# A two-layer hybrid decoder trunk on one core: the next layer's norm one step behind its residual, table transfers with weight loads between them, the norm row loaded ahead of the constants, and a new order of jobs

## The chip, the core and the metric

The kernel runs on one core of a Trainium2 chip. A core has five engines that each execute their own list of instructions in order: TensorE (PE, matmuls; PEld in the rows is its weight load), VectorE (DVE), ScalarE (ACT), GpSimd (POOL) and SyncE (SP), which here only issues DMA transfers, all in one queue. The metric is the device time of one execution in microseconds, as the median of several runs.

## The reference

Two layers, 512 tokens, 1024 channels. Each layer normalises its input, projects it with one wide matrix `w_in`, feeds five token mixers, gates and sums them, projects with `w_out`, normalises once more and adds the result to its input:

```python
def layer(x, mem, pos, l):                          # cut to its structure
    h = rms_norm(x, norm_pre[l])
    a, b, c, d, q, gates = split(h @ w_in[l], IN_SIZES)
    y = [rwkv7_branch(a), dsa_branch(b, pos), retention_branch(c, pos),
         s5_branch(d), cross_attention(q, mem)]
    m = sum(sigmoid(g_i) * (y_i @ w_branch[l, i]) for i, ...)
    return x + rms_norm(m @ w_out[l], norm_post[l])
```

All of it is float32. The S5 branch is a diagonal complex recurrence, y = scan over t of s = lambda * s + B u; its powers of lambda are a table that depends on the weights alone.

## The kernel before, in words

Every weight matrix is streamed in pieces of 128 x 512 numbers (256 KB), 448 of them. A piece (`class Load`) is brought by SP into `raw` (5 buffers), ACT casts it to a rounded high part `wh` (4 buffers), DVE makes the rest `wl = raw - wh` (4 buffers, called the split), and PE does three matmuls for each product: high by high, low by high, high by low. Activations are held the same way, as `hh` and `hl`. `prefetch` issues transfers up to 5 pieces ahead and casts and splits up to 3 pieces ahead of the job that uses them, in the order of use.

The products are jobs with short names (`rq`, `xq`, `dv` and so on). `ORDER` (L40) lists them for each of the two layers; the mixers between them run as generators in lanes, with priorities in `LANES` (L42). When the program is built, `run()` steps through jobs and lanes with a model of the engines' clocks (`Sched`, constants `LAG`, `EARLY`, `ADD_G`) and so fixes the order in which each engine gets its instructions; on the chip nothing is reordered. A `yield` in a generator is a place at which `run()` may go on with something else.

Where layer 0 goes over to layer 1, `out_jobs` multiplies by `w_out` for tokens 0 to 255 and then 256 to 511. For each of the four tiles of 128 tokens `finish_out` makes the residual (`x<-ou,ors,x`, two halves on DVE, behind a power `ors` on POOL) and calls `put_hT` for the next layer: the sum of squares on ACT (`xn<-x`), a power on POOL (`xrs`), two products on DVE (`xn<-x,xrs,npre`), eight transposes on PE, `hh` on ACT and `hl` on DVE. The new input is also stored (`xs<-x`). Jobs of layer 1 that need only two tiles (`rq`, `rk`, `xq`, `rv`) run as half jobs as soon as these are there; a half job takes its pieces twice as fast as a whole one.

`s5_tables` makes the S5 tables of a layer. `sar` grows by doubling, seven times, with `sta`, `sea`, `seb`, `sem` as helpers; each group of three operations goes to DVE or POOL, whichever the model thinks free (`free_for`), the rest to POOL. Then four transfers `s5tab<-sar` and four loads of `sBt` go out on SP, and the loads of `sCg` follow. SP issues in order, so a transfer whose data is not there holds every later one, the weight pieces too.

At the start SP loads `x` of token tile 0, the first constants `cst`, `x` of tile 1, the norm's row `npre`, and then the first five weight pieces. `first_h` runs `put_hT` for the four tiles.

Of the kernel before, what the change touches and what calls it, by code (L numbers as in the profile page):

```python
# [31 lines left out]
CW2 = float(np.float32(np.round((TWO_PI - CW1) * 2.0 ** 21) / 2.0 ** 21))  # L32
CW3 = float(np.float32(TWO_PI - CW1 - CW2))
MAGIC = 12582912.0
LAG = 11.5
EARLY = -1.0
MAXL = 6
NBUF = {"c1": 10, "c2": 14, "c4": 16, "c16": 2, "raw": 5, "w": 4}
ADD_G = 1.2
ORDER = ("rsg rv w wg g0 xq xsg di su dsg ssg dq g4 g2 dk mem1 dv g3 mem g1",  # L40
         "xsg dq g0 w di rsg wg g4 su dsg ssg dk dv g3 g1 g2")
LANES = ("ret idx>4 s5>4 ms1>3 rwkv dsa ms0 tab x>2", "idx>4 dsa>0 tab ret x rwkv>t s5")  # L42


def shape_constants():
# [177 lines left out]
def hybrid_kernel(ctx: ExitStack, tc: tile.TileContext, x, mem, positions, norm_pre, norm_post, norm_mem, w_in,  # L223
# [17 lines left out]
    def psb(shape=(128, 512)):  # L241
        return sched.ring("b", 5, pp.tile(list(shape), F32, name="b", tag="b", bufs=5))


    def sb(name, shape, dt=F32, bufs=2, lane="c", big=False):
        n = int(np.prod(shape[1:]))
        if n <= 128 and not big:
            return bp.tile(list(shape), dt, name=name, tag=name, bufs=bufs)
        if dt == BF16:
            return bp.tile([128, 512], dt, name=name, tag="m1", bufs=3)  # L250
        if n == 4096 and dt == F32:
            return sched.ring("mg", 1, bp.tile(list(shape), dt, name=name, tag="mg", bufs=1))
        c, w = next((c, w) for c, w in ((1, 256), (2, 516), (4, 1032), (16, 4096)) if n <= w and not (big and c == 1))
        t = bp.tile([128, w], dt, name=name, tag=f"c{c}", bufs=NBUF[f"c{c}"])
        v = t[:shape[0], :n]
        if len(shape) > 2:
            names = "abcdef"[:len(shape) - 1]
            v = v.rearrange(f"p ({' '.join(names)}) -> p {' '.join(names)}",
                            **{m: k for m, k in zip(names, shape[1:])})
        return v  # L260

    def f32(ap):
        return ap.bitcast(F32)

    def bcast_row(ap, name):

        t = sb(name, [128, ap.shape[-1]])
        SY.dma_start(t, bass.AP(tensor=ap.tensor, offset=ap.offset, ap=[[0, 128], [1, ap.shape[-1]]]))
        return t
# [6 lines left out]
    def load_x(l, i):  # L276
        t = sb("x", [128, D])
        SY.dma_start(t, xr[:, i, :] if l == 0 else xs[:, i, :])
        return t

    x0 = [load_x(0, 0)]
    ncst = COFF["qdec"][0]
    cst = cp.tile([128, ncst], F32, name="cst")
    nci = COFF["ident"][1]
    assert COFF["ident"][0] == 0 and CONST.shape[1] == ncst + 1024
    SY.dma_start(cst[:, :nci], const[:, :nci])
    x0.append(load_x(0, 1))
    npre = {0: bcast_row(norm_pre[0], "npre")}

    def K(n):  # L290
        o, w = COFF[n]
# [6 lines left out]
    def rsq(dst, src):  # L298
        sh = list(src.shape)
        assert len(sh) == 2  # L300
        G.tensor_tensor(dst, src, mhalf[:sh[0], :sh[1]], op=OP.pow)
# [147 lines left out]
    def rms_scale(src, name, j):  # L449

        r = sb(name, [128, 1], bufs=4)
        A.activation(j, src, AF.Square, accum_out=r)
        V.tensor_scalar(r, r, 1.0 / D, 1e-6, op0=OP.mult, op1=OP.add)
        rsq(r, r)
        return r
# [27 lines left out]
    def new_hT(l):  # L483
        hh = sb("hh", [128, 8, S], F32R)
        hl = sb("hl", [128, 8, S], F32R)
        hT[l] = (hh, hl)

    def put_hT(l, i, xi):

        if l not in hT:  # L490
            new_hT(l)
        hh, hl = hT[l]
        xn = sb("xn", [128, D])
        r = rms_scale(xi, "xrs", xn)
        yield
        for o in (slice(0, 512), slice(512, 1024)):
            V.scalar_tensor_tensor(xn[:, o], xi[:, o], r, npre[l][:, o], op0=OP.mult, op1=OP.mult)
        yield
        for k in (0, 4):
            ps = psb((128, 4, 128))  # L500
            for kk in range(4):
                T.transpose(ps[:, kk, :], xn[:, 128 * (k + kk):128 * (k + kk) + 128], ident)
            o = (slice(None), slice(k, k + 4), slice(128 * i, 128 * i + 128))
            A.copy(hh[o], ps)
            V.tensor_tensor(hl[o], ps, f32(hh[o]), op=OP.subtract)
            yield
# [25 lines left out]
    def prefetch(upto, ahead=2):  # L532

        while len(stream) < upto + NBUF["raw"] and select():
            pass
        while lp["dma"] < min(len(stream), upto + NBUF["raw"]):
            stream[lp["dma"]].dma()
            lp["dma"] += 1
        while lp["split"] < min(lp["dma"], upto + 1 + ahead):
            stream[lp["split"]].split()  # L540
            lp["split"] += 1
# [54 lines left out]
    def select():  # L596

        left = [jb for jb in jobs if not jb.taken]
        if not left:
            return False  # L600
        lanes = [q.room for q in queue if have(q.need)][:1]

        def last(jb):
            return jb.merge is not None and sum(m == jb.merge for m in merging) == 4

        def fits(jb, spare=()):
            if jb.gate is not None and jb.gate[1] == 0 and opened:
                return False
            return room_for({"c4": 6} if last(jb) else jb.room, spare)
        if any(not t.granted for t in begun):  # L610
            return False
        able = [j for j in left if (j.after is None or j.after.taken) and have(j.need)
                and not (opened and j.gate is not None and j.gate[1] == 0)]
        jb = next((j for j in able if fits(j, lanes)), None)
        if jb is None and able:
            jb = able[0]
            if last(jb) or not all(have(q.need) for q in active):
                return False
            jb.granted = False
        elif jb is None:  # L620
            jb = left[0]
            if not fits(jb, lanes) and (active or not fits(jb)):
                return False
        jb.last = last(jb)
        begun[:] = [t for t in begun if not t.granted] + [jb]
        if jb.granted:
            grant(jb)
        if jb.merge is not None:
            merging.append(jb.merge)
        if jb.gate is not None:  # L630
            opened[:] = [jb.gate[0]] if jb.gate[1] < 3 else []
        jb.taken = True
        for w in jb.loads:
            w.idx = len(stream)
            stream.append(w)
        taken.append(jb)
        return True
# [792 lines left out]
    def s5_tables(l):  # L1430
# [5 lines left out]
        tab = [area[:, r_] for r_ in range(2)]  # L1436
# [12 lines left out]
        while m < 128:  # L1449
# [3 lines left out]
            t = tmp[:, :, :m]  # L1453
# [12 lines left out]
        for r_ in range(2):  # L1466
            for b in range(2):
                SY.dma_start(s5d["tab"][2 * l + b][:, r_], tab[r_][:, 4 * b:4 * b + 4].rearrange("p b m -> p (b m)"))

        Bt = sb("sBt", [128, 2, nb, 16])  # L1470
        Cs = sb("sCs", [128, 2, nb, 16])
        for r_, w in enumerate((s5_b_re, s5_b_im)):
            bv = w[l].rearrange("(b q) p c -> q p b c", q=2)
            for q in range(2):
                SY.dma_start(Bt[64 * q:64 * q + 64, r_], bv[q])
        yield
        for b in range(2):
# [46 lines left out]
        for b in range(2):  # L1524
# [23 lines left out]
            for j in range(4):  # L1548
                for i in range(j, 4):
                    n = 32 * (3 - (i - j))  # L1550
# [228 lines left out]
    def finish_out(l, i):  # L1779

        u, rr, xi = (a[i % 2] for a in ST[l, "fin", i // 2])
        rs = sb("ors", [128, 1])
        V.tensor_tensor(rs, rr[:, 0:1], rr[:, 1:2], op=OP.add)
        V.scalar_tensor_tensor(rs, rr[:, 2:3], 16e-6, rs, op0=OP.add, op1=OP.add)
        rsq(rs, rs)
        yield
        for a in range(2):
            o = slice(512 * a, 512 * a + 512)
            V.scalar_tensor_tensor(xi[:, o], u[:, o], rs, xi[:, o], op0=OP.mult, op1=OP.add)
            if l == L - 1:  # L1790
                yield
                SY.dma_start(outr[:, i, o], xi[:, o])
        if l < L - 1:
            yield from put_hT(l + 1, i, xi)
            SY.dma_start(xs[:, i, :], xi)

# [30 lines left out]
    def run(lanes, maxl=MAXL):  # L1827
# [3 lines left out]
        while alive or active or queue:  # L1831
# [9 lines left out]
            now = sched.clock["pe"]  # L1841
            late = max(sched.clock["dve"], sched.clock["act"]) > now + LAG
            pick = None if late and alive else next(
# [53 lines left out]
    def first_h(i):  # L1897
        if i >= 2:
            x0.append(load_x(0, i))
            yield  # L1900
        yield from put_hT(0, i, x0[i])

    lanes = [Lane(lambda i=i: first_h(i), ("t01",) if i > 1 else (), f"t0{i}", c4=2 + (i == 0)) for i in range(4)]
    lanes += [Lane(setup, ("t01",), "setup", c2=3, c4=4)]
    for l in range(L):
# [31 lines left out]
        }  # L1937
        for n in ORDER[l].split():
            if n[0] == "g":
                gate_jobs(l, int(n[1]))  # L1940
            else:
# [10 lines left out]
                    "dsa": Lane(lambda l=l: branch_dsa(l), (f"dsa_q{l}", "trig"), f"y{l}1", c1=2, c2=5, c4=2)}  # L1952
        for n in LANES[l].split():
            n, _, after = n.partition(">")
# [39 lines left out]
```

## Time and profile before

| | |
|---|---|
| median of 3 runs | 1432.06 us (1430.72 to 1433.5) |
| the profiled execution's own time | 1431.76 us |
| its span, first to last instruction | 1430.0 us |
| mean granted clock of TensorE | 0.986 of full speed |
| PE busy | 1373.7 us, 96% of the span |
| DVE busy | 950.2 us, 66% |
| ACT busy | 558.3 us, 39% |
| POOL busy | 279.1 us, 20% |
| HBM traffic | 114 GB/s over the span |

The profiled execution took 1.76 us more than its span. Busy times are sums over an engine's instructions; that PE is busy does not say at which of its two clocks (1.2 or 2.4 GHz) it ran, which the granted clock tells. Times in the rows are us from the first instruction.

### The profile page before, as it was taken

The numbers are of one execution on the slowest core, as the hardware profiler recorded it, in microseconds if no ns is written. First come the engines' busy times: TensorE is split into PE (matmuls) and PEld (weight loads), VectorE is DVE, ScalarE is ACT, GpSimd is POOL, SyncE is SP. The second block draws the span as 40 slices with busy tenths as digits, with TensorE's granted clock in tenths as the row PEclk, the third lists the DMA queues.
The fourth block names the chain that finished last, engine by engine and source line by source line (L and its number), as shares of the span: only waits on it lengthen the run. The fifth ranks groups of instructions, "written<-read, shape, count | busy, mean of one in ns | idle before, by whom it ended". The sixth has DMA issues, their size and how long they took to land.

```text
span 1430.0 us, 21718 instructions
## 1 busy us (share of the span) xinstructions
PE 1373.7 (96%) x7774; PEld 1147.8 (80%) x7774; DVE 950.2 (66%) x2027; ACT 558.3 (39%) x1196; POOL 279.1 (20%) x329
## 2 busy tenths in 40 slices
PE   5999999999999999999979899999999999999997
PEld 5878777788878887888979788687888788778887
DVE  5677565978867864444666567668788786844465
ACT  5433445333334235233554452443323332344353
POOL 0194241000111111110019523210010112411000
PEclk9999899999999999999999899999999999999999
DMA  6644425364242432344656624263534322422355
GB/s 193 176 114 127 122 89 141 89 184 126 72 121 74 129 101 52 89 118 125 188 152 177 180 78 134 60 143 94 141 103 147 89 67 72 114 67 81 99 163 181
DMA packets 243414, 170.60 MB, mean 119 GB/s; under 512 B 27657, under 2 KB 228331, under 8 KB 243307
## 3 DMA queue, kind: packets, MB, share of 16 engines
q1 hardware_dynamic: 243307, 169.22, 42.6%
q8 instruction: 61, 1.00, 0.3%
q14 instruction: 46, 0.38, 0.1%
HBM read 144.53 MB, written 18.87 MB: 114 GB/s over the span
## 4 chain that ended last, share of the span: by engine, by line
PE 82%; DVE 6%; POOL 4%; DMA 3%; ACT 2%; issue 2%; SPq 1%; POOLq 0%; DVEq 0%; ACTq 0%
PE d L209 62%; PE b L209 19%; DVE wl L209 2%; POOL sar L209 2%; DMA raw<-in_w_out_dram 1%; POOL sta L209 1%; DMA raw<-in_w_in_dram 1%; DVE x L209 1%; SPq L209 1%; ACT wh L209 0%; DMA posi<-in_positions_dram 0%; DMA x<-in_x_dram 0%; DMA rsw<-rq 0%; POOL sem L209 0%; POOL rsw L209 0%
## 5 line engine op out<-in xcount | busy, mean ns | idle before, releaser
L209 PE MATMUL d<-hh,wh 128*128 128x512 f32 (+2 forms) x1232 | 488.3, 396 | 13.5 <-ACT wh L209 13.5
L209 PE MATMUL d<-hh,wl 128*128 128x512 f32 (+2 forms) x1232 | 474.3, 385 | 6.6 <-DVE wl L209 6.5
L209 PE MATMUL d<-hl,wh 128*128 128x512 f32 (+2 forms) x1232 | 472.1, 383 | 0.0
L209 DVE TENSOR_TENSOR wl<-raw,wh 128x512 fp32r<-128x512 f32 x448 | 334.0, 761 | 139.2 <-ACT wh L209 135.6
L209 ACT CAST wh<-raw 128x512 fp32r<-128x512 f32 x448 | 268.7, 617 | 165.6 <-PE d L209 111.9
L209 PEld LDWEIGHTS d<-hh,wh 128*128 128x128 f32 (+1 forms) x1232 | 235.6, 191 | 73.1 <-issue 15.0
L209 PEld LDWEIGHTS d<-hh,wl 128*128 128x128 f32 (+1 forms) x1232 | 234.8, 191 | 58.4 <-DVE wl L209 10.1
L209 PEld LDWEIGHTS d<-hl,wh 128*128 128x128 f32 (+1 forms) x1232 | 235.8, 191 | 42.3 <-issue 0.5
L209 POOL TENSOR_TENSOR mg<-mg,gth 128x512 f32<-128x512 f32 x48 | 69.9, 1457 | 486.2 <-DVE gth L209 486.2
L209 DVE SCALAR_TENSOR_TENSOR gth<-gth,d 128x512 f32<-128x512 f32 x64 | 43.9, 686 | 107.2 <-PE d L209 103.4
L209 ACT ACTIVATE gth<-d 128x512 f32<-128x512 f32 (+1 forms) x90 | 51.9, 577 | 159.7 <-PE d L209 155.0
L209 PE MATMUL b<-wh,mgs 128*128 128x256 f32 x320 | 63.2, 283 | 5.6 <-ACT wh L209 4.1
L209 PE MATMUL d<-yl,wh 128*128 128x512 f32 x160 | 62.9, 393 | 0.7 <-DVE yl L209 0.7
L209 PE MATMUL d<-yh,wl 128*128 128x512 f32 x160 | 62.8, 393 | 0.0
L209 PE MATMUL d<-yh,wh 128*128 128x512 f32 x160 | 62.7, 392 | 0.0
L209 PEld LDWEIGHTS b<-wh,mgs 128*128 128x128 f32 x320 | 52.1, 190 | 6.3 <-ACT wh L209 4.3
L209 DVE MAX8 dm<-dac 128x8 f32<-128x256 f32 (+2 forms) x96 | 52.8, 550 | 0.1
L209 DVE MATCH_REPLACE8 dac<-dm,dac 128x256 f32<-128x256 f32 (+2 forms) x96 | 52.1, 543 | 0.0
L209 PE MATMUL b<-wl,mgs 128*128 128x256 f32 x160 | 45.5, 285 | 0.3 <-DVE wl L209 0.3
L209 POOL TENSOR_TENSOR ors<-ors,mhalf 128x1 f32<-128x1 f32 x8 | 5.0, 634 | 203.3 <-DVE ors L209 203.3
L209 PE MATMUL d<-wh,mgs 128*128 128x256 f32 x192 | 40.6, 285 | 2.0 <-DVE ou L209 2.0
L209 POOL TENSOR_TENSOR rsw<-rsw,sinT 128x1024 f32<-128x1024 f32 (+1 forms) x12 | 29.7, 2480 | 44.0 <-DMA rsw<-diq 20.7
(399 smaller groups left out, 2067.9 us busy)
## 6 DMA issues: line engine op xcount, KB each, us to landing
raw<-in_w_in_dram SPq DMA_DIRECT2D x324, 256.0 KB, 3.4
raw<-in_w_out_dram SPq DMA_DIRECT2D x64, 256.0 KB, 4.7
raw<-in_w_branch_dram SPq DMA_DIRECT2D x40, 256.0 KB, 3.2
x<-in_x_dram SPq DMA_DIRECT2D x8, 512.0 KB, 6.0
raw<-in_w_mem_kv_dram SPq DMA_DIRECT2D x16, 256.0 KB, 2.9
s5tab<-sar SPq DMA_DIRECT2D x8, 256.0 KB, 2.0
s5Wi<-sar SPq DMA_DIRECT2D x4, 512.0 KB
nn<-wNt SPq DMA_DIRECT2D x8, 256.0 KB
```

The source lines that it names most:

```text
L209: r = f(*args, **kw)
```

## The change

The module constants `LAG`, `ORDER` and `LANES` get other values, by which nearly every engine's order changes somewhere. In `s5_tables` a `yield` follows each pair of table transfers and stands ahead of each `sBt` load. In `finish_out` a `yield` stands between the residual and the norm of the next layer. At the start `npre` is loaded ahead of `cst`, and `first_h` calls `prefetch(0, 0)` in the second step of tile 1.

```diff
@@ -32,14 +32,14 @@
 CW2 = float(np.float32(np.round((TWO_PI - CW1) * 2.0 ** 21) / 2.0 ** 21))
 CW3 = float(np.float32(TWO_PI - CW1 - CW2))
 MAGIC = 12582912.0
-LAG = 11.5
+LAG = 10.5
 EARLY = -1.0
 MAXL = 6
 NBUF = {"c1": 10, "c2": 14, "c4": 16, "c16": 2, "raw": 5, "w": 4}
 ADD_G = 1.2
-ORDER = ("rsg rv w wg g0 xq xsg di su dsg ssg dq g4 g2 dk mem1 dv g3 mem g1",
-         "xsg dq g0 w di rsg wg g4 su dsg ssg dk dv g3 g1 g2")
-LANES = ("ret idx>4 s5>4 ms1>3 rwkv dsa ms0 tab x>2", "idx>4 dsa>0 tab ret x rwkv>t s5")
+ORDER = ("xq rsg rv w g1 wg g3 xsg dsg di ssg su g4 dk dq dv mem1 mem g2 g0",
+         "w xsg g1 dq di rsg dv g0 ssg su g3 g4 wg dk g2 dsg")
+LANES = ("ms1>3 tab ms0 s5 dsa>2 ret x rwkv idx>4", "ret s5>2 rwkv>4 x tab dsa>0 idx>2")
 
 
 def shape_constants():
@@ -279,13 +279,13 @@
         return t
 
     x0 = [load_x(0, 0)]
+    npre = {0: bcast_row(norm_pre[0], "npre")}
     ncst = COFF["qdec"][0]
     cst = cp.tile([128, ncst], F32, name="cst")
     nci = COFF["ident"][1]
     assert COFF["ident"][0] == 0 and CONST.shape[1] == ncst + 1024
     SY.dma_start(cst[:, :nci], const[:, :nci])
     x0.append(load_x(0, 1))
-    npre = {0: bcast_row(norm_pre[0], "npre")}
 
     def K(n):
         o, w = COFF[n]
@@ -1466,12 +1466,14 @@
         for r_ in range(2):
             for b in range(2):
                 SY.dma_start(s5d["tab"][2 * l + b][:, r_], tab[r_][:, 4 * b:4 * b + 4].rearrange("p b m -> p (b m)"))
+            yield
 
         Bt = sb("sBt", [128, 2, nb, 16])
         Cs = sb("sCs", [128, 2, nb, 16])
         for r_, w in enumerate((s5_b_re, s5_b_im)):
             bv = w[l].rearrange("(b q) p c -> q p b c", q=2)
             for q in range(2):
+                yield
                 SY.dma_start(Bt[64 * q:64 * q + 64, r_], bv[q])
         yield
         for b in range(2):
@@ -1791,6 +1793,7 @@
                 yield
                 SY.dma_start(outr[:, i, o], xi[:, o])
         if l < L - 1:
+            yield
             yield from put_hT(l + 1, i, xi)
             SY.dma_start(xs[:, i, :], xi)
 
@@ -1898,7 +1901,10 @@
         if i >= 2:
             x0.append(load_x(0, i))
             yield
-        yield from put_hT(0, i, x0[i])
+        for n, _ in enumerate(put_hT(0, i, x0[i])):
+            if n == 1 and i == 1:
+                prefetch(0, 0)
+            yield
 
     lanes = [Lane(lambda i=i: first_h(i), ("t01",) if i > 1 else (), f"t0{i}", c4=2 + (i == 0)) for i in range(4)]
     lanes += [Lane(setup, ("t01",), "setup", c2=3, c4=4)]
```

Three places show what this moves. The first is SP's queue at the layer seam: `raw` are weight pieces, `xs` the stored residuals, `s5tab` and `sBt` the table transfers and loads. Before:

```order
L209 DMA raw<-in_w_in_dram 128x4x128 x12
L209 DMA raw<-in_w_in_dram 128x2x256
L209 DMA xs<-x 128x1024 x2
L209 DMA raw<-in_w_in_dram 128x2x256 x3
L209 DMA raw<-in_w_in_dram 128x4x128 x11
L209 DMA s5tab<-sar 128x512 x4
L209 DMA sBt<-in_s_b_re_dram 64x8x16 x2
L209 DMA sBt<-in_s_b_im_dram 64x8x16 x2
L209 DMA raw<-in_w_in_dram 128x4x128
```

And now, from the same place in the program:

```order
L209 DMA raw<-in_w_in_dram 128x4x128 x8
L209 DMA raw<-in_w_in_dram 128x2x256 x3
L209 DMA xs<-x 128x1024
L209 DMA raw<-in_w_in_dram 128x2x256
L209 DMA xs<-x 128x1024
L209 DMA raw<-in_w_in_dram 128x4x128 x10
L209 DMA s5tab<-sar 128x512 x2
L209 DMA raw<-in_w_in_dram 128x4x128 x2
L209 DMA s5tab<-sar 128x512 x2
L209 DMA raw<-in_w_in_dram 128x2x256 x3
L209 DMA sBt<-in_s_b_re_dram 64x8x16
L209 DMA raw<-in_w_in_dram 128x2x256
```

Before, 27 pieces of `w_in` went out ahead of the four table transfers and none between them or the `sBt` loads. Now 26 go out ahead of the first pair (2 and 2 stand ahead of these rows), two between the pairs, three behind the second, and further ones between the `sBt` loads.

On POOL the same place begins with the power `ors` of the second half's residual; the steps of the table follow. Before:

```order
L209 TENSOR_TENSOR ors<-ors,mhalf 128x1 x2
L209 MEMSET sar 128x8 x2
L209 COPY sem<-un 128x16
L209 TENSOR_TENSOR xrs<-xrs,mhalf 128x1 x2
L209 TENSOR_TENSOR sar<-sar,sem 128x8
L209 TENSOR_TENSOR sta<-sar,sem 128x8
L209 TENSOR_TENSOR sar<-sar,sta 128x8
L209 TENSOR_TENSOR sea<-sem 128x16
L209 TENSOR_TENSOR seb<-sem 128x8 x2
```

And now:

```order
L209 COPY sem<-un 128x16
L209 TENSOR_TENSOR sar<-sar,sem 128x8
L209 TENSOR_TENSOR sta<-sar,sem 128x8
L209 TENSOR_TENSOR sar<-sar,sta 128x8
L209 TENSOR_TENSOR sea<-sem 128x16
L209 TENSOR_TENSOR seb<-sem 128x8 x2
L209 TENSOR_TENSOR sem_7221<-sea 128x8
L209 TENSOR_TENSOR sem_7221<-seb 128x8
L209 TENSOR_TENSOR xrs<-xrs,mhalf 128x1 x2
L209 TENSOR_TENSOR sar<-sar,sem_7221 128x8x2
```

Eight steps of the table, from `sar` to `sem`, moved from behind the two `xrs` powers to ahead of them. Of the next doubling one group of three steps, which was POOL's, stands on DVE now.

On DVE, at the residual of tiles 0 and 1 (the first half of the seam), `wl` is the split of a weight piece and `xrs` prepares the norm's power. Before:

```order
L209 SCALAR_TENSOR_TENSOR ors<-or,ors 128x1
L209 TENSOR_TENSOR wl<-raw,wh 128x512 x2
L209 SCALAR_TENSOR_TENSOR x<-ou,ors,x 128x512 x2
L209 TENSOR_SCALAR xrs<-xrs 128x1
L209 SCALAR_TENSOR_TENSOR x<-ou,ors,x 128x512 x2
L209 TENSOR_SCALAR xrs<-xrs 128x1
L209 TENSOR_TENSOR wl<-raw,wh 128x512 x3
L209 SCALAR_TENSOR_TENSOR xn<-x,xrs,npre 128x512 x4
```

And now:

```order
L209 TENSOR_TENSOR wl<-raw,wh 128x512 x2
L209 SCALAR_TENSOR_TENSOR x<-ou,ors,x 128x512 x4
L209 TENSOR_TENSOR wl<-raw,wh 128x512 x2
L209 TENSOR_SCALAR xrs<-xrs 128x1
L209 TENSOR_TENSOR wl<-raw,wh 128x512
L209 TENSOR_SCALAR xrs<-xrs 128x1
L209 TENSOR_TENSOR wl<-raw,wh 128x512
L209 SCALAR_TENSOR_TENSOR xn<-x,xrs,npre 128x512 x2
L209 TENSOR_TENSOR ou<-b,npost 128x512
L209 TENSOR_TENSOR ou<-d,npost 128x512
L209 TENSOR_TENSOR wl<-raw,wh 128x512
L209 SCALAR_TENSOR_TENSOR xn<-x,xrs,npre 128x512 x2
```

The two residuals stand together ahead of both `xrs`, and four splits (before, three behind them) stand between the residuals and the first norm product.

## Rows read from the trace of the kernel before

**Rows 1.** The page: busy time, share of span and instructions of each engine.

```profile
PE 1373.7 (96%) x7774; PEld 1147.8 (80%) x7774; DVE 950.2 (66%) x2027; ACT 558.3 (39%) x1196; POOL 279.1 (20%) x329
```

**Rows 2.** Waits of PE by what it waited for: total us, times, longest us.

```profile
PE d L209 <- ACT wh L209: 13.5, 4, 8.4
...
PE d L209 <- DVE wl L209: 7.2, 7, 2.2
```

**Rows 3.** Windows: length, busy us (instructions) per engine, then PEclk, DMA share, GB/s.

```profile
160.00:170.00 10.00, 10.00 (x35) 8.74 (x36) 4.50 (x7) 4.66 (x13) 4.94 (x2) 0.50 0.29 80
...
200.00:204.00 4.00, 4.00 (x14) 3.17 (x15) 2.06 (x5) 3.66 (x12) 3.80 (x6) 0.59 0.00 0
...
720.00:740.00 20.00, 19.27 (x152) 19.07 (x153) 15.38 (x27) 11.01 (x28) 0.00 (x0) 0.93 0.67 201
740.00:760.00 20.00, 16.79 (x128) 16.38 (x128) 14.74 (x30) 10.54 (x22) 12.45 (x35) 0.91 0.58 172
...
788.00:798.00 10.00, 6.03 (x27) 5.81 (x28) 4.12 (x5) 3.54 (x7) 5.34 (x9) 0.50 0.98 267
```

**Rows 4.** Timeline of SP, 700 to 800: start, us, operation, tile, count.

```profile
752.49 21.66 SPq L209 DMA_DIRECT2D raw<-in_w_in_dram  x14
779.86 5.05 SPq L209 DMA_DIRECT2D s5tab<-sar  x4
...
787.81 2.66 SPq L209 DMA_DIRECT2D raw<-in_w_in_dram  x5
```

**Rows 5.** Timeline of POOL, 740 to 790: in brackets idle time before, and releaser.

```profile
742.05 0.20 POOL L209 COPY sem<-un 128x16 f32<-128x16 f32 x1
746.75 0.98 POOL L209 TENSOR_TENSOR xrs<-xrs,mhalf 128x1 f32<-128x1 f32 x1 [4.50 <-DVE xrs L209]
749.44 0.55 POOL L209 TENSOR_TENSOR xrs<-xrs,mhalf 128x1 f32<-128x1 f32 x1 [1.71 <-DVE xrs L209]
749.95 0.52 POOL L209 TENSOR_TENSOR sar<-sar,sem 128x8 f32<-128x8 f32 x1
...
755.00 0.20 POOL L209 TENSOR_TENSOR sem<-seb 128x8 f32<-128x8 f32 x1
...
782.81 1.28 POOL L209 TENSOR_TENSOR sar<-sar,sta 128x512 f32<-128x512 f32 x1
```

**Rows 6.** Timeline of PE, 715 to 795, the rows with a wait.

```profile
719.15 0.38 PE L209 MATMUL b<-wh,mgs 128*128 128x256 f32 x1 [4.15 <-ACT wh L209]
719.87 0.58 PE L209 MATMUL b<-wl,mgs 128*128 128x256 f32 x1 [0.34 <-DVE wl L209]
...
749.73 0.39 PE L209 MATMUL d<-hh,wh 128*128 128x256 f32 x1 [2.99 <-ACT wh L209]
...
791.97 0.58 PE L209 MATMUL d<-hh,wh 128*128 128x256 f32 x1 [8.35 <-ACT wh L209]
```

**Rows 7.** Timeline of DVE at the first wait.

```profile
712.69 0.69 DVE L209 TENSOR_TENSOR wl<-raw,wh 128x512 fp32r<-128x512 f32 x1 [2.56 <-ACT wh L209]
713.30 1.41 DVE L209 SCALAR_TENSOR_TENSOR x<-ou,ors,x 128x512 f32<-128x512 f32 x2
```

**Rows 8.** Timeline of PE in layer 0, 155 to 199.

```profile
157.00 1.61 PE L209 MATMUL b<-wwa,lora 64*128 64x512 f32 x4 [1.09 <-ACT sar L209]
...
191.36 1.89 PE L209 MATMUL b<-xvm,xpT 128*128 128x64 f32 x16
...
195.86 0.50 PE L209 MATMUL d<-hh,wl 128*128 128x512 f32 x1 [0.89 <-DVE wl L209]
...
198.50 1.95 PE L209 MATMUL b<-cst,wr 128*128 128x2 f32 x16 [0.57 <-DVE xon L209]
```

**Rows 9.** Timelines of ACT, DVE and PE at the start.

```profile
7.65 1.06 ACT L209 ACTIVATE xn<-x 128x1024 f32<-128x1024 f32 x1 [1.98 <-DMA x<-in_x_dram]
...
9.11 2.74 DVE L209 SCALAR_TENSOR_TENSOR xn<-x,xrs,npre 128x512 f32<-128x512 f32 x4
...
15.32 0.58 PE L209 MATMUL d<-hh,wh 128*128 128x256 f32 x1 [1.19 <-ACT wh L209]
```

## The prediction

> **What bounds the kernel now.** I began with the page. TensorE (PE) is busy for 1373.7 of 1430.0 us [rows 1], so whatever the new order does to VectorE (DVE), ScalarE (ACT) or GpSimd (POOL) counts only where PE waits for it, or where PE works at the slower of its two clocks (1.2 instead of 2.4 GHz). The two programs hold the same matmuls, so nothing is to be had from the work itself. The list of PE's waits by releaser came next: its largest entries, behind the start, are waits for `wh`, the cast half of a weight piece, 13.5 us in 4 waits of which one alone is 8.4, and for `wl`, 7.2 us in 7 [rows 2]. The timeline puts three large ones at the layer seam: 4.15 us before 719.15 and 2.99 us before 749.73, where the residuals of token tiles 0, 1 and of 2, 3 are made, and 8.35 us before 791.97 [rows 6]. I call them the first, second and third wait. Windows then showed where the clock is low: 0.50 over 160 to 170 and over 788 to 798, where PE was busy for 6.03 of the 10 us, 0.59 over 200 to 204, and 0.93 and 0.91 around the first two waits [rows 3]. One us of work at the low clock costs 0.5 us.
>
> What makes the third wait is seen on SyncE (SP), which issues all transfers in one queue. Fourteen weight pieces went out in 21.66 us from 752.49 (about 1.5 us each), then SP stood until the table transfers of 779.86, whose four issues ended at 784.91; four `sBt` transfers followed, and the next piece left at 787.81 [rows 4]. SP stood because the table was not there: POOL's chain of doubling steps ended at 784.09 (782.81 + 1.28) [rows 5]. That chain began at 742.05, but then sat behind the two `xrs` powers of the norm, which were waiting for DVE, until 749.95 [rows 5].
>
> **The change part by part.**
>
> *Table transfers and chain.* (a) Eight steps (from `sar` at 749.95 to `sem`, ending 755.20) now stand ahead of the two `xrs`. They took 5.2 us, about 0.66 each, beside DVE's splits and norm products, although the last of them alone took 0.20 [rows 5]. Even at 0.66 they fit into the 4.50 and 1.71 us in which POOL idled [rows 5]. The chain goes on behind the second `xrs`, at 749.99, with its ninth step. Upper bound: the following steps run at 0.2, all 5.2 us are saved, and a group of three steps that goes to DVE saves 0.6 more: 5.8. Lower bound: the steps that take the freed place run beside the same splits and products and stretch the same way; then only 8 x 0.2 + 0.6 = 2.2 is gained. I take 2.2, since DVE's work behind the second `xrs` is as dense as before. (b) The weight pieces no longer stand behind `sBt`: 787.81 - 784.91 = 2.9 us. (c) The first pair of tables goes out after 26 pieces instead of 27, two pieces go before the second pair, and so one more piece reaches PE before the last hold: 1.5 us of work. Sum 2.2 + 2.9 + 1.5 = 6.6 us, and some 1.8 us of the 8.35 are left. What PE saves in the second wait arrives here as waiting, since the chain is counted from the same residual; I cost the second wait at nothing by itself (bounds 0 and 2.99). (d) After a remaining wait of two or so us I expect a low-clock stretch like that after the second wait, the 0.91 of 740 to 760, 20 x 0.09 = 1.8 us, instead of 6.03 x 0.5 = 3.0 [rows 3]: -1.2. Together -7.8.
>
> The same rows meet a rule that speaks against (a). The Trainium skill, page "SBUF — State Buffer", section "Who interferes with whom", says that a DVE instruction with two SBUF inputs contends with a GpSimd instruction that reads SBUF, and that whoever comes first holds the pair for the whole instruction. The trace agrees for POOL (0.66 beside DVE, 0.20 alone). By the rule the residual products, which have two such inputs, would in turn be held by the eight steps now beside them, 8 x 0.2 = 1.6 us; the chain would start again that much later, and the sum would be 1.6 us smaller, 1422.2. The rows can't show it, as no step stood there.
>
> *Norm one step behind its residual.* At the first wait DVE now does all four residual products before anything else. Before, the split ending at 713.38 was followed by two products of together 1.41 us, a wait for ACT's square and two more products, and PE, back at 719.15, still waited 0.34 us for the next split [rows 6, 7]. Now ACT casts six pieces ahead of its squares, and DVE's third split comes straight behind 2.8 us of products: ready at about 713.3 + 2.8 + 0.7 = 716.8. PE stopped at 719.15 - 4.15 = 715.0 and so waits 1.8 us: the gain is 4.15 + 0.34 - 1.8 = 2.7. Bounds: 0, if the norm, now behind more splits, makes PE's transposes late; 4.5 if nothing waits. The clock's 0.93 over 720 to 740 [rows 3] cost 20 x 0.07 = 1.4 us; whether it falls after the shorter wait is open, 0 to 1.4, and I take half, 0.7. At the second wait nine splits now lie between the residual and the last `hl`, where five lay, and PE takes the transposes of tiles 2 and 3 two pieces later: cover of 3 us for 4 x 0.69 = 2.8 [rows 7], so this costs nothing unless that cover is missing; then up to 2.8 us.
>
> *New order of jobs.* In layer 0 the small matmuls of RWKV, S5 tables and cross-attention fall together differently. Before: waits of 1.09, 0.89 and 0.57 us [rows 8], a window at 0.50 (5.0 us lost) and one at 0.59 (4 x 0.41 = 1.6) [rows 3]: 9.2 in all. The clock fell there beside PE busy throughout 160 to 170, after a stretch of short matmuls with single waits of about 1 us. Now there are two such clusters with no weight matmul inside. The longer holds `xp` twice, `xvm` twice, `xkm`, `wv`, `wr` and `wta`; at what the 16 matmuls of `xvm` (1.89) and of `wr` (1.95) took [rows 8], and half of that for each group of eight, that is near 10 us. The shorter is half as long. Costed like the two seen, 5.0 + 1.6, and with half the waits, 1.3 us, that is 7.9: -1.3. The page "TensorE: Matmul & The Clock Gate" of the Trainium skill, section "HAM oscillation", ties the return to the low clock to waits between matmuls. By that rule alone the long cluster would keep its clock and the sum would be 5.0 us better; the row at 157.00 shows the fall after 1.09 us, so the trace does not bear that out. The other places where lanes now meet cost something unknown: the rest of PE's waits for `wl` is 7.2 - 2.2 = 5 us [rows 2], so -5 to +5, and I put +1.
>
> *Head.* The norm row `npre` is loaded ahead of the constants, but DVE still handles `xrs` of tile 1 before the `xn` products of tile 0, and tile 1 now arrives last. The products, before at 9.11 [rows 9], thus move by up to the 1.5 us that now lie between the start of tile 1's square at 7.65 and them [rows 9]. In return the first piece is cast and split ahead of `hh` and `hl`; PE waited 1.19 us for it [rows 9]. I cost the head at 0 (bounds -1.2, +1.5).
>
> Sum: -7.8 - 2.7 - 0.7 - 1.3 + 1 + 0 = -11.5. The profiled execution took 1431.76 us (1430.0 of span and 1.76 around it), so 1420.3; the median of the runs lies 0.3 us above it: **1420.6 us**.
>
> **The rivals.** 0.2%, what a measurement can tell from no change here, is 2.9 us: faster means under 1429.2, slower over 1434.9.
>
> *The third wait goes entirely.* If the chain gains 5.8 instead of 2.2, the pieces arrive in time: then 8.35 + 3.0 and about 1.5 of the second wait go, 12.9 instead of 7.8, and the time is about 1415.5. For it: POOL's steps at 0.20. Against: the 0.66 beside DVE.
>
> *The new order eats part.* If the clusters of layer 0 cost twice what I put (7.9 more), or layer 1 opens a few waits of the size of rows 8, 1425 to 1429; with both, 1429 to 1435, no change that can be measured. For it: the gain is an order's, and the same order moves every branch. Against: all seven waits for `wl` together are 7.2 us [rows 2].
>
> *Slower.* In layer 0 the clusters now lie within some 50 us of PE work. If the clock, once fallen, doesn't recover between them, each us of that work costs one us more. The forecast has 6.6 us there; from about 11.5 + 2.9 + 6.6 = 21 us of work at 1.2 GHz on, the kernel is slower than before; all 50 would give about 1464. For it: both falls of before lie in this stretch. Against: each ended within 10 us, as soon as weight matmuls ran.
>
> *The edits don't do what they say.* The head may not move at all (DVE's order there is unchanged), and the pairs of tables may still hold the queue as long as four did, if the chain gains nothing: -4.4 for (b) and (c) instead of -6.6, 1422.8. Both lie inside the forecast's range.
>
> **How the numbers follow.** Forecast, 1417 to 1425: 0.45. Third wait gone, 1411 to 1417: 0.18, and below 1411: 0.03. Part eaten, 1425 to 1429.2: 0.15. Wholly eaten, to 1434.9: 0.10. Slower: 0.09. So faster 0.81, same 0.10, slower 0.09. The range 1411 to 1431 leaves out 0.03 below, and above it 0.09 and about half of the 0.10: 0.17 in all.
>
> **What would show it.** On SP the four table transfers stand in two rows with two pieces between, and the piece behind the second pair leaves about 5 us earlier relative to the second residual; PE's wait there is 1 to 3 us instead of 8.35. POOL has eight steps before the second pair of `xrs`, the chain ends 2 to 3 us earlier; 5 or more would be the first rival. The first wait reads 1 to 2.5 us. Windows over 140 to 210 show one long and one short low-clock stretch; a third, or one over 15 us, is the slow rival. The forecast is wrong in its mechanism if the chain ends no earlier and the third wait still goes, or if PE waits for `hl` or the transposes of tiles 2 and 3.

## The result, and the profile after

The changed kernel takes **1413.16 us** (median of 4 runs, 1412.35 to 1413.86) against 1431.39 us before in the same comparison: a ratio of 0.9877, 95% interval 0.9851 to 0.9904. It is faster by some 18 us, where 11.5 were forecast. The profiled execution spans 1410.6 us. Its page, first the span and then busy time by engine:

```profile
span 1410.6 us, 21729 instructions
...
PE 1363.8 (97%) x7774; PEld 1139.6 (81%) x7774; DVE 940.1 (67%) x2022; ACT 557.9 (40%) x1196; POOL 285.5 (20%) x334
```

PE is busy for 9.9 us less than in [rows 1] with as many matmuls: that part is the clock. The rest of the 19.4 us by which the span is shorter is waiting. Its list of waits (total us, times, longest), to be held against [rows 2]:

```profile
PE d L209 <- DVE wl L209: 7.4, 10, 1.6
PE d L209 <- ACT wh L209: 4.4, 4, 1.7
PE d L209 <- DVE ou L209: 3.5, 2, 1.9
```

The waits for `wh` went from 13.5 to 4.4 us, those for `wl` stayed in sum, in ten smaller pieces. The waits for `ou`, into which DVE reads out the products with `w_out`, grew. The longest of them lies at the seam; first before, then now:

```profile
732.31 0.39 PE L209 MATMUL d<-wh,mgs 128*128 128x256 f32 x1 [0.73 <-DVE ou L209]
...
723.10 0.38 PE L209 MATMUL d<-wh,mgs 128*128 128x256 f32 x1 [1.89 <-DVE ou L209]
```

The three waits of the seam, in PE's timeline, answer to [rows 6]:

```profile
711.27 0.39 PE L209 MATMUL b<-wl,mgs 128*128 128x256 f32 x1 [1.27 <-DVE wl L209]
...
737.38 0.38 PE L209 MATMUL d<-hh,wl 128*128 128x256 f32 x1 [1.57 <-DVE wl L209]
...
772.15 0.39 PE L209 MATMUL d<-hh,wh 128*128 128x256 f32 x1 [1.66 <-ACT wh L209]
```

4.15 became 1.27, 2.99 became 1.57, 8.35 became 1.66. SP at the third of them, to be held against [rows 4]:

```profile
766.91 0.82 SPq L209 DMA_DIRECT2D s5tab<-sar  x2
767.83 1.00 SPq L209 DMA_DIRECT2D raw<-in_w_in_dram  x2
771.16 0.81 SPq L209 DMA_DIRECT2D s5tab<-sar  x2
772.07 1.49 SPq L209 DMA_DIRECT2D raw<-in_w_in_dram  x3
773.61 0.69 SPq L209 DMA_DIRECT2D sBt<-in_s_b_re_dram  x1
```

The wait of 1.66 us is for the two pieces between the pairs, which left at 767.83; those behind the second pair, at 772.07, came in time. POOL's chain, against [rows 5]; its first row, `ors`, stood in the kernel before at

```profile
740.96 1.06 POOL L209 TENSOR_TENSOR ors<-ors,mhalf 128x1 f32<-128x1 f32 x2 [21.56 <-DVE ors L209]
```

and stands now at

```profile
731.63 1.07 POOL L209 TENSOR_TENSOR ors<-ors,mhalf 128x1 f32<-128x1 f32 x2 [17.95 <-DVE ors L209]
...
732.72 0.20 POOL L209 COPY sem<-un 128x16 f32<-128x16 f32 x1
...
738.78 1.49 POOL L209 TENSOR_TENSOR xrs<-xrs,mhalf 128x1 f32<-128x1 f32 x2
740.24 0.21 POOL L209 TENSOR_TENSOR sar<-sar,sem 128x16 f32<-128x16 f32 x1
...
769.86 1.27 POOL L209 TENSOR_TENSOR sar<-sar,sta 128x512 f32<-128x512 f32 x1
```

From the copy of `sem` to the chain's end there were 42.0 us before (742.05 to 784.09); now there are 38.4 (732.72 to 771.13). The `xrs` powers stand behind the first steps. The windows show where the clock still falls (columns as in [rows 3]):

```profile
150.00:160.00 10.00, 7.25 (x46) 6.84 (x46) 6.04 (x24) 4.87 (x14) 0.40 (x1) 0.83 0.21 75
...
180.00:190.00 10.00, 9.41 (x41) 7.05 (x40) 7.45 (x12) 7.16 (x18) 8.98 (x7) 0.87 0.15 30
...
212.00:230.00 18.00, 17.71 (x142) 15.25 (x141) 10.62 (x21) 9.59 (x28) 2.62 (x4) 1.00 0.20 53
...
690.00:740.00 50.00, 44.37 (x368) 43.32 (x367) 39.12 (x84) 30.23 (x72) 10.79 (x19) 1.00 0.64 188
740.00:780.00 40.00, 38.12 (x306) 37.58 (x305) 25.84 (x32) 19.79 (x40) 30.27 (x59) 0.96 0.77 211
```

The first two waits cost no clock any more (1.00 over 690 to 740), the third 40 x 0.04 = 1.6 us. In layer 0, behind 100 us, two low windows are left, at 0.83 and 0.87 over 10 us each; they cost 3.0 us, where the windows at 0.50 and 0.59 cost 5.0 + 1.6 [rows 3]. Over 212 to 230, where the long cluster of small matmuls lies, the clock is full.

One row splits the span in three: the first and the last start of the `w_out` matmuls `b<-wh,mgs` (the three numbers ahead of these are their least, median and largest duration in ns). First the kernel before, then the changed one:

```profile
L209 PE MATMUL b<-wh,mgs x320: 276/281/416, 682.7 to 1408.2; 128*128 128x256 f32 x160
...
L209 PE MATMUL b<-wh,mgs x320: 274/280/388, 677.5 to 1388.5; 128*128 128x256 f32 x160
```

So layer 0 with the head is 5.2 us shorter, seam and layer 1 are 14.5 us shorter (725.5 to 711.0), and the rest is 0.3 us longer.

### The profile page after: what moved, and what is told of

Its sections match the earlier page's. It is cut to its first block, busy times and chain, and to the rows that moved or that the text cites. A ratio compares the mean times of both kernels' runs of the same rounds, so it can differ in the third digit from the quotient of the medians.

```text
span 1410.6 us, 21729 instructions
## 1 busy us (share of the span) xinstructions
PE 1363.8 (97%) x7774; PEld 1139.6 (81%) x7774; DVE 940.1 (67%) x2022; ACT 557.9 (40%) x1196; POOL 285.5 (20%) x334
## 4 chain that ended last, share of the span: by engine, by line
PE 85%; DVE 5%; ACT 3%; DMA 2%; POOL 2%; issue 2%; SPq 0%; DVEq 0%; POOLq 0%; ACTq 0%
PE d L209 66%; PE b L209 20%; DVE wl L209 1%; POOL sar L209 1%; DMA raw<-in_w_in_dram 1%; DMA raw<-in_w_out_dram 1%; POOL sta L209 1%; DVE wL L209 1%; ACT wh L209 0%; DMA posi<-in_positions_dram 0%; DMA x<-in_x_dram 0%; DVE xmx L209 0%; ACT sTp L209 0%; POOL seb L209 0%; SPq L209 0%
## 5 line engine op out<-in xcount | busy, mean ns | idle before, releaser
L209 POOL TENSOR_TENSOR mg<-mg,gth 128x512 f32<-128x512 f32 x48 | 66.7, 1390 | 463.4 <-DVE gth L209 463.4
```

What stands on the lines that cost most here:

```text
L209: r = f(*args, **kw)
```

## The experiments

The change has four parts: the yields of `s5_tables` (tables), the yield ahead of `put_hT` (norm), load order and early prefetch at the start (head), and the constants (order). Four kernels make one part alone, four undo one. After the first result my theory was that the parts add up; its rival, for each pair of parts, that they work only together. The first four ran beside the kernel before (1431.4 us there), the other four beside it on another chip (1431.02 us) and without the changed kernel, so that each is compared by its ratio to the kernel before on its own chip.

**Tables alone.** A yield behind each pair of `s5tab` transfers and one ahead of each `sBt` load:

```diff
+            yield
...
             for q in range(2):
+                yield
                 SY.dma_start(Bt[64 * q:64 * q + 64, r_], bv[q])
```

> The kernel before with the new yields of s5_tables alone. Local theory (each edit pays where its own rows stand): the weight pieces leave the queue ahead of the sBt loads (2.9 us) and one more piece reaches PE before the last table pair (1.5 us); the chain itself gains nothing, since its steps still stand behind the two xrs. The third wait falls from 8.35 to about 4 us, and the time by 4 to 6 us, to about 1426. Rival (the edits work only together): the chain still ends as late, so the pieces between the pairs come no earlier, the wait stays over 6 us and the time falls by less than 2.5 us.

1425.73 us, ratio 0.9959 (0.9945 to 0.9974), 5.7 us less. The third wait fell further than I had put: PE's row has 1.76 us.

```profile
783.72 0.39 PE L209 MATMUL d<-hh,wh 128*128 128x256 f32 x1 [1.76 <-ACT wh L209]
```

On SP the first pair went out as soon as its half of the table was there, 4.2 us before the chain's end (782.70), and took the two pieces with it:

```profile
778.46 0.82 SPq L209 DMA_DIRECT2D s5tab<-sar  x2
779.38 1.01 SPq L209 DMA_DIRECT2D raw<-in_w_in_dram  x2
782.72 0.81 SPq L209 DMA_DIRECT2D s5tab<-sar  x2
783.63 1.48 SPq L209 DMA_DIRECT2D raw<-in_w_in_dram  x3
```

So the pairs and what stands between them do not need the chain to be earlier: from `ors` to its end it took 42.3 us here (740.39 to 782.70), and 43.1 in the kernel before. I had taken the chain's end as the gate for every piece; the half that is ready 4 us earlier is the gate for the first two.

**Norm alone.**

```diff
         if l < L - 1:
+            yield
             yield from put_hT(l + 1, i, xi)
```

> The kernel before with the yield between residual and norm alone. Local theory: the first wait falls from 4.15 + 0.34 to about 1.3 us and keeps its clock (4 to 5 us together); eight table steps run ahead of the xrs powers, the chain ends some 3.6 us earlier after ors, but now only 25 pieces stand ahead of the four tables instead of 27, so the third wait stays at 7 to 8 us. Time about 1425 to 1427. Rival (together only): first wait as in the changed kernel, third wait over 9 us, time within 2.5 us of before.

1424.2 us, 0.9949 (0.9935 to 0.9964), 7.2 us less. The first wait is gone (no wait over 0.5 us there), the second is 1.54, and the third is longer than before, and than the 7 to 8 us that I expected:

```profile
779.83 0.58 PE L209 MATMUL d<-hh,wh 128*128 128x256 f32 x1 [9.48 <-ACT wh L209]
```

Some of what the first two waits give up arrives at the third as waiting, although the chain ends 771.97 - 732.91 = 39.1 us after `ors` begins, 4 us less than in the kernel before. A third wait over 9 us was a sign that I had set for the rival; its other sign, a time within 2.5 us of before, did not come.

**Head alone, order alone.**

```diff
     x0 = [load_x(0, 0)]
+    npre = {0: bcast_row(norm_pre[0], "npre")}
...
     x0.append(load_x(0, 1))
-    npre = {0: bcast_row(norm_pre[0], "npre")}
...
-        yield from put_hT(0, i, x0[i])
+        for n, _ in enumerate(put_hT(0, i, x0[i])):
+            if n == 1 and i == 1:
+                prefetch(0, 0)
+            yield
```

```diff
-LAG = 11.5
+LAG = 10.5
...
-ORDER = ("rsg rv w wg g0 xq xsg di su dsg ssg dq g4 g2 dk mem1 dv g3 mem g1",
+ORDER = ("xq rsg rv w g1 wg g3 xsg dsg di ssg su g4 dk dq dv mem1 mem g2 g0",
...
-LANES = ("ret idx>4 s5>4 ms1>3 rwkv dsa ms0 tab x>2", "idx>4 dsa>0 tab ret x rwkv>t s5")
+LANES = ("ms1>3 tab ms0 s5 dsa>2 ret x rwkv idx>4", "ret s5>2 rwkv>4 x tab dsa>0 idx>2")
```

> The kernel before with npre ahead of the constants and the early prefetch alone. Local theory: first matmul with weights at 14.5 instead of 15.3, PE without the wait of 1.19 us, low clock until about 15.3 instead of 19.8: 2.5 to 3 us less, about 1429. Rival (the head is hidden by later waits): the wait for wl at 33 to 38 us takes what the head gains, time within 1 us of before.

> The kernel before with the new LAG, ORDER and LANES alone. Local theory: layer 0 up to the first w_out matmul 2 to 3 us shorter, three low-clock stretches of 3.4 us in place of 6.8, 10.2 and 3.4; the seam as before with 8.35 us of third wait; layer 1 unchanged within 1 us. Time about 1428 to 1430. Rival (the order is what pays): 6 us or more less, with a third wait under 5 us.

Neither moves the time: 1432.12 us, 1.0001 (0.9984 to 1.0018), and 1432.09 us, 1.0011 (0.9997 to 1.0024). My expectation of 2 to 3 us for each was wrong. Tables and norm alone, if they add up, thus make 12.9 of the 18.2 us, and 5 are left.

**One part undone.** The same hunks, taken out of the changed kernel one at a time. First tables, then norm:

```diff
                 SY.dma_start(s5d["tab"][2 * l + b][:, r_], ...)
-            yield
...
-                yield
                 SY.dma_start(Bt[64 * q:64 * q + 64, r_], bv[q])
```

```diff
         if l < L - 1:
-            yield
             yield from put_hT(l + 1, i, xi)
```

For the head both of its hunks go back, for the order the three constants:

```diff
-    npre = {0: bcast_row(norm_pre[0], "npre")}
...
-                prefetch(0, 0)
```

```diff
-LAG = 10.5
+LAG = 11.5
...
-ORDER = ("xq rsg rv w g1 wg g3 xsg dsg di ssg su g4 dk dq dv mem1 mem g2 g0",
+ORDER = ("rsg rv w wg g0 xq xsg di su dsg ssg dq g4 g2 dk mem1 dv g3 mem g1",
```

> The changed kernel without the new yields of s5_tables: 26 pieces, four tables, four sBt, then weights. Additive theory: the third wait comes back at about 9.5 us, as in a_norm, since the norm edit makes PE reach it earlier than the chain ends, with a low-clock stretch of 7 to 10 us behind it: 8 to 11 us slower than the changed kernel, 1421 to 1424. Rival (the earlier chain alone feeds the pieces in time): third wait under 4 us, 1415 to 1417.

> The changed kernel without the yield ahead of the norm. Additive theory: first wait 3.6 to 4.2, second 3.0 to 3.3, each followed by 3.4 us at the low clock, chain 3 to 4 us later after ors, third wait 1.5 to 2.5 as in a_tables: 6 to 9 us slower than the changed kernel, 1419 to 1422. Rival (table and norm edits share one gain): over 10 us slower, third wait over 4.

> The changed kernel with the old load order and without the early prefetch. Additive theory after a_head, which gained nothing: within 2 us of the changed kernel, first matmul with weights at 14.4 to 15.3, two waits of about 1 us at 33 to 38 back. Rival (the head is worth what the changed kernel's trace shows, 2.7 us): 2 to 4 us slower.

> The changed kernel with the old LAG, ORDER and LANES. Additive theory after a_order, which gained nothing: within 2 us of the changed kernel, layer 0 up to the first w_out matmul within 2 us. Rival (the order pays once the seam waits are gone): 3 to 6 us slower, with the low-clock stretches of layer 0 of before.

The medians and, from the same row as above, the first and last `w_out` start in the profiled execution:

| kernel | median us | ratio to before (95%) | first start | first to last |
|---|---|---|---|---|
| before | 1431.39 | | 682.7 | 725.5 |
| changed | 1413.16 | 0.9877 (0.9851 to 0.9904) | 677.5 | 711.0 |
| tables alone | 1425.73 | 0.9959 (0.9945 to 0.9974) | 682.0 | 720.5 |
| norm alone | 1424.2 | 0.9949 (0.9935 to 0.9964) | 680.1 | 719.3 |
| head alone | 1432.12 | 1.0001 (0.9984 to 1.0018) | 681.8 | 726.4 |
| order alone | 1432.09 | 1.0011 (0.9997 to 1.0024) | 681.4 | 724.7 |
| tables undone | 1422.09 | 0.9926 (0.9902 to 0.995) | 676.4 | 716.0 |
| norm undone | 1420.1 | 0.9921 (0.99 to 0.9943) | 679.9 | 715.8 |
| head undone | 1422.28 | 0.9938 (0.9915 to 0.996) | 688.8 | 711.0 |
| order undone | 1420.18 | 0.992 (0.9893 to 0.9947) | 682.2 | 713.6 |

At the seam the parts nearly add up: tables are worth 5.0 us alone and 5.0 in the changed kernel (last column), norm 6.2 and 4.8, the order 0.8 and 2.6, the head -0.9 and nothing. Made alone they sum to 11.1 us, undone to 12.4, of 14.5; the column is of one execution each, and no run shows what the other 2 to 3 us are. With the tables undone the third wait is back, at 8.38 us, while with the norm undone the first is 2.59 (I expected 3.6 to 4.2), the second 3.26 and the third 1.71. The rivals at the seam are out as they were put: with the norm undone the third wait stays under 4 us and the loss under 10, and the earlier chain alone does not feed the pieces in time.

In layer 0 they do not add up (first starts are of one execution each and scatter by some us, but the medians say the same). Head and order alone bring 0.9 and 1.3 us there, together 5.2 (3.7 between the means of the three kernels that have neither and of the three that have both); undoing the head loses 11.3 us, undoing the order 4.7. For both the additive theory falls. Nor is the loss with the head undone one of the new order with the old head as such: order alone has these two as well, and its first start is 681.4, not 688.8. The two differ ahead of `w_out` by the yields in `s5_tables`, which layer 0 runs through too, and PE's order parts at 109 us. With the new head, taking these yields out leaves layer 0 its order. As far as one trace of each shows, the slow layer 0 thus takes the new order, the new yields and the old head together.

The loss with the head undone is not at the head. Most of it lies at two places. At 172 us PE waits for a split:

```profile
177.18 0.80 PE L209 MATMUL d<-hh,wl 128*128 128x512 f32 x1 [4.70 <-DVE wl L209]
```

DVE was at four small products and then at the split itself, each stretched while POOL worked beside it (in the changed kernel the four take 1.14 us, an undisturbed split 0.69):

```profile
170.23 4.26 DVE L209 SCALAR_TENSOR_TENSOR sTp<-cst,pv,sTp 128x128 f32<-128x128 f32 x4 [2.81 <-ACT sTp L209]
...
175.43 1.70 DVE L209 TENSOR_TENSOR wl<-raw,wh 128x512 fp32r<-128x512 f32 x1
```

```profile
171.62 2.12 POOL L209 TENSOR_TENSOR sm<-pout,sCs 128x512 f32<-128x512 f32 x2
173.71 1.53 POOL L209 TENSOR_SCALAR sm<-sm 128x512 f32<-128x512 f32 x1
175.32 1.26 POOL L209 TENSOR_TENSOR sar<-sm 64x512 f32<-64x512 f32 x1
```

And over 212 to 230 a cluster of small matmuls runs at the low clock (0.53, where the changed kernel has 1.00):

```profile
212.00:230.00 18.00, 17.98 (x69) 13.42 (x69) 13.54 (x23) 5.38 (x18) 4.64 (x6) 0.53 0.01 1
```

**Which part of the head.** The last four ran on one chip, the changed kernel itself among them.

```diff
     x0 = [load_x(0, 0)]
-    npre = {0: bcast_row(norm_pre[0], "npre")}
...
     x0.append(load_x(0, 1))
+    npre = {0: bcast_row(norm_pre[0], "npre")}
```

> The changed kernel with npre behind the constants again, the early prefetch kept; layer 0 gets another order (some 2000 rows of PE's differ), much as without both head edits. Planner theory: 5 to 9 us slower, lost between the first weight matmul and the first w_out matmul, with waits and low-clock stretches at 150 to 235 that the changed kernel does not have. Direct theory: within 1.5 us, the head itself being as early.

```diff
-        for n, _ in enumerate(put_hT(0, i, x0[i])):
-            if n == 1 and i == 1:
-                prefetch(0, 0)
-            yield
+        yield from put_hT(0, i, x0[i])
```

> The changed kernel without the early prefetch, npre still ahead of the constants; layer 0 keeps its order but for two rows. Direct theory (the head edit pays at the head): a wait of 1.2 us or more ahead of the first weight matmul and the low clock there some 3 us longer, 2 to 3 us slower. Planner theory (the head edit's worth lies in the order of layer 0 that the model makes of it): under 1.5 us slower.

> The changed kernel once more, beside the next three on one chip. If the time differs between executions only by where the low clock falls, it stays within 1410 to 1419 and its executions order themselves by their mean granted clock.

The changed kernel repeated at 1413.33 us (1411.2 to 1417.22). With `npre` behind the constants it takes 1422.76 us, 9.4 more, although PE then starts on the weights earlier, at 13.22 us against 14.69 in the changed kernel on this chip:

```profile
13.22 0.56 PE L209 MATMUL d<-hh,wh 128*128 128x256 f32 x1
```

The earlier row thus makes the first weight matmul 1.5 us later, which is the bound I had given. It is not a loss for long. 192 weight matmuls on, at the first `d<-hh,wh` of 128x512, the kernel with `npre` behind the constants is the later one, 47.92 us against 46.85, after a wait of 2.05 us for a split (before 34.68) and the low clock over 35 to 39 (0.57). And the first `w_out` matmul comes at 687.8 instead of 677.5, with the same two losses as with both head edits undone (4.76 us of wait before 176.84, low clock from 212 on). The planner theory holds: what the row brings is another order of layer 0, because the order is made with a model of when each engine is free, and the new `ORDER` and `LANES` fit that start. Without the prefetch the time is 1417.52 us, 4.2 us more. The weights start 1.4 us later (16.08), of which 0.3 are left at the same 128x512 matmul (47.19) and 0.9 at the first `w_out` matmul (678.4). Most of the rest lies at the third wait, 4.40 us instead of 1.64, where now 24 pieces instead of 26 stand ahead of the tables. That is again the plan, so neither theory was right about its size.

**A version that might beat both: the first pair later.**

```diff
         yield
+        for _ in range(2 if l else 0):
+            yield
         for r_ in range(2):
...
             for b in range(2):
                 SY.dma_start(s5d["tab"][2 * l + b][:, r_], ...)
```

> The changed kernel with two more yields of the table lane of layer 1 ahead of the first table pair: 28 weight pieces go out ahead of it instead of 26, nothing else of the order moves but a few rows. Queue theory (PE's third wait is SP standing in front of a table that is not ready): the wait of 1.66 us falls under 0.5, its low-clock stretch of 3.4 us goes too, the time falls by 2 to 3.5 us, and the chain on POOL ends when it did. Rival (the wait only moves behind the second pair, whose data is ready 4 us later): a wait of over 1 us some 5 us later, same time within 1 us.

1414.88 us (1409.87 to 1418.46) beside 1413.33: no difference that can be told. The queue theory holds at its place, the third wait is 0.55 us and without a low clock, but another wait grew, some 30 us further on and thus not behind the second pair, as the rival had it:

```profile
776.40 0.39 PE L209 MATMUL d<-wh,hh 128*128 128x256 f32 x1 [0.55 <-ACT wh L209]
...
803.74 0.50 PE L209 MATMUL d<-hh,wl 128*128 128x512 f32 x1 [2.59 <-DVE wl L209]
```

The low clock over 804 to 815 followed. That split stood on DVE behind a product of 3.43 us, which in the changed kernel took 1.22; POOL's product of 2.40 us ran beside it here:

```profile
798.79 3.43 DVE L209 TENSOR_TENSOR rq<-rq,cosT 128x1024 f32<-128x1024 f32 x1
```

```profile
798.74 2.40 POOL L209 TENSOR_TENSOR rsw<-rsw,sinT 128x1024 f32<-128x1024 f32 x1 [1.30 <-DMA rsw<-rk]
```

In the changed kernel the two meet as well, but there the split is the one stretched, to 2.88 us, and PE waits 0.59 us. What moved is the order in which the two engines met. No version here beats the changed kernel.

## Why the prediction held, and where its terms were off

*The third wait (forecast -7.8).* The mechanism was right in its outline: pieces held in SP's queue, freed by pairs and by `sBt` behind weights. That 1.66 us are left where 1.8 were forecast is partly luck, for two terms of the sum were wrong and offset each other. I took the chain's end as the gate of every piece. With the tables alone, where the chain ends hardly earlier, the wait is already 1.76: pairs and `sBt` are worth 6.6 us there, not the 4.4 of (b) and (c). And the earlier chain, whose gain is 3.6 us (43.1 to 39.5 from `ors` to the end) instead of 2.2, inside its bounds, does not shorten the wait, because PE comes to it sooner by as much: 38.9 us after `ors`, 42.7 in the kernel before, 41.6 with the tables alone. What PE saves at the second wait therefore does not come back as waiting at the third. I cost it at nothing, "since the chain is counted from the same residual", but 1.4 us of that wait and its low clock were saved. The clock's term (d) was right: 1.6 us where 1.8 were put.

Seam and layer 1 together: forecast 11.2 (7.8 + 2.7 + 0.7), measured 14.5. With the clock costed as the prediction does it, the rows give 6.7 + 3.0 - 1.6 = 8.1 for the third wait, 3.2 + 1.4 = 4.6 for the first, 1.4 + 1.8 = 3.2 for the second, and -1.2 for the longer wait for `ou`: 14.7. What the forecast lacked is above all the second wait. By the table 0.8 to 2.6 of the 14.5 come with the order; these rows do not tell where.

*The first wait (-2.7 and -0.7).* Right: 1.27 us with no second wait for a split right behind it, and full clock. The split behind the four products ended at 711.2 where they began at 707.9, 3.3 us later, about as reckoned. What I did not see is the price of the norm's new place: the wait for `ou`, 0.73 us before, is 1.89 in the changed kernel and with the norm alone, and 0.91 with the norm undone.

*Layer 0 and head (-1.3, +1, 0).* This is the step that failed: forecast 0.3 us, measured 5.2 (3.7 between the means above). I put the head at 0, with the wait of 1.19 us as its only gain, and added head and order up as separate terms. At its place the head is worth more. The first `d<-hh,wh` of 128x512, before and now:

```profile
50.67 0.40 PE L209 MATMUL d<-hh,wh 128*128 128x512 f32 x1
...
46.76 0.39 PE L209 MATMUL d<-hh,wh 128*128 128x512 f32 x1
```

In the five traces with the old head this matmul starts at 47.6 to 50.7 us, in the seven with both new edits at 46.6 to 47.5. The waits of 2.17 and 1.34 us for splits before 35.43 and 38.55, and the low clock over 36 to 44, which the kernel before has there, did not enter my sum. Head alone is 3.2 us ahead at this matmul and has 0.9 us left at the first `w_out`. So behind it the terms are not separate: head and order are each worth nothing in the whole when made alone, and the head changes which order the program gets.

And I put 5.0 us of low clock on the long cluster, "costed like the two seen". It kept the full clock; its longest wait is 0.29 us. The low windows at 150 and 180 come behind waits of 1.34 and 1.42 us (before 152.73 and 154.64) and of 1.47 us (before 177.48), and with the head undone its cluster fell behind a wait of 0.61. The rule of the Trainium skill that I set aside ("TensorE: Matmul & The Clock Gate", "HAM oscillation": waits between matmuls bring the low clock back) fits these rows in kind, though the waits of its example, 3 to 5 us, are longer. But with the order alone the clock fell with PE busy throughout, in a cluster of small matmuls, as I had feared for this one:

```profile
170.00:198.00 28.00, 28.00 (x163) 22.18 (x162) 16.99 (x34) 14.31 (x35) 13.53 (x12) 1.00 0.45 123
198.00:202.00 4.00, 4.00 (x16) 2.83 (x16) 3.86 (x8) 1.23 (x3) 2.66 (x1) 0.57 0.00 0
```

What decides whether such a cluster keeps its clock stays open.

*The rivals.* The time lies in the range of 1411 to 1431, but below the forecast's own 1417 to 1425. It is among those that I gave to "the third wait goes entirely", but not for that reason: the wait is there. Of the 7.9 us by which the profiled execution fell below the sum, 4.9 came from layer 0 and the head, and 3.3 from seam and layer 1, with 0.3 lost behind. The slow rival did not come; no low-clock stretch of layer 0 in the changed kernel is longer than 7 us.

## What to carry to other kernels

A transfer whose data comes late belongs in an in-order queue only behind what the busy engine needs until then; where it can be cut into parts that are ready at different times, the pieces between the parts are free (5 us here, with nothing computed earlier). Where a build-time model sets the order, an edit's own cost and its effect on the plan are two things: here a load order that made the first weight matmul 1.5 us later was worth 9 us in the whole, and the head's edits, 3 us ahead at their place, were worth nothing in the end with the old table of jobs. Undo an edit as well as making it alone before saying what it brings.

## What the runs showed of the hardware

The low clock follows short waits, but not always, and it can come without one (198 to 202 with the order alone, above). In the changed kernel a wait of 1.47 us before 177.48 was followed by a low-clock stretch of 3.4 us, the longer ones before 723.10 (1.89 us) and 737.38 (1.57) by none; the same wait of 1.89 us had one in the kernel with the head undone. Executions of one kernel differ by it: the six of the changed kernel on one chip lie between 1411.2 us at a mean granted clock of 0.994 and 1417.22 at 0.989, and stand in the order of their clocks but for two neighbours. Differences of 0.3% between two profiles of such a kernel can be this alone, so parts of that size were judged by medians of several executions.

DVE and POOL hold each other up in both directions. POOL's small steps took 0.66 us beside DVE's two-input work and 0.20 alone [rows 5]; DVE's product `rq` took 3.43 us where it started 0.05 us behind POOL's `rsw`, and 1.22 where it started 0.04 us ahead of it; there `rsw` took 3.43 instead of 2.40, and the split behind `rq` 2.88 instead of an undisturbed 0.69. As the Trainium skill has it ("SBUF — State Buffer", "Who interferes with whom"), whoever issues first holds the pair of ports that the two share for the whole instruction. The trace agrees. It also shows the price that I could not take from the rows of before: small POOL steps cost DVE nothing (in the changed kernel four residual products took 2.73 us at 707.89 with POOL idle, and 2.73 at 733.99 beside the table's steps), so the 1.6 us that I reckoned by that rule did not come; a POOL product of 1024 columns cost it 2 us.
